# Five edits to a two-layer decoder trunk: order of the gate exponents, masks of the attention scores, last feed-forward chunk, first weight pieces, planned costs

## The chip, the cores and the metric

The kernel runs on one core of one Trainium2 chip. The metric is the device time of one execution in microseconds (us). A measurement of this kernel repeats to a few tenths of a microsecond: three runs of the kernel before gave 2133.31, 2133.43 and 2133.77 us.

## The reference

Input x is 256 tokens by 2048 features in float32. There are two layers. Each computes x + W_out(mixer(RMSNorm(x) W_in)) and then x + squared-ReLU MLP(RMSNorm(x)) with 8192 hidden features.

Layer 0's mixer is sparse attention with 16 heads of 128 in 4 groups. A query sees three branches: 15 compressed blocks of keys, selected blocks (with 256 tokens every block is selected, so this is plain causal attention) and a window (causal as well). Each branch has its own masked softmax, and a gate weighs the three.

Layer 1's mixer is gated linear attention (GLA) with 4 heads, 256 keys and 512 values per head:

```
log_a = log_sigmoid(g_lr @ w_gate_up + b_gate) / 16
decay = exp(cum_i - cum_j)        # cum: running sum of log_a, per key feature, j <= i
att   = einsum('id,jd,ijd->ij', q, k, decay);   o = att @ v  (+ state of earlier chunks)
o     = rms_norm(o) * silu(r)
```

## The kernel before, in words

**Precision.** Every large product is done with operands split into a high and a low fp32r part (hi, lo): hi·hi + hi·lo + lo·hi. For a piece of weights of 128 x 1024, ScalarE writes the high part (`copy`, L197, tile wh) and VectorE the low part (`tt`, L201, tile wl). TensorE multiplies with 512 columns at a time (`mm`, L166).

**Order of the work.** One stream of TensorE instructions is written out by the program: projections, feed-forward chunks, output projections. Weights come in halves; `Weights.next` (L491) splits up to three halves ahead of the one in use. All the small work in between (norms, softmax, decays, evacuations) lives in generators, "streams", that a planner steps. `Plan` (L34) keeps a modelled time per engine; each helper adds a planned cost (for example `free * 1.042 + 75` ns for a VectorE tensor_tensor). After each matmul `W.tick` (L98) goes through the streams in the order in which they were spawned and lets each that is ready emit its next step, unless ScalarE or VectorE is modelled over 3.2 us ahead of TensorE. `W.drain` and `W.wait` (L109, L116) step streams with no such bound until a stream is done or a buffer is free. Instructions are emitted in that order and each engine executes its own in order, so a planned cost that is too low makes TensorE wait at a product whose operand is late.

**NSA scores.** `attend` (L1331) handles one head: token tile 0 gets one PSUM tile of 272 columns (128 selected, 128 window, 16 compressed), token tile 1 one of 256 and one of 272. `score` (L1339) makes three products per tile and, for the two tiles of 272, a fourth, identity times mask, that adds 0 or -1e30. `largest` (L1358) takes the negated row maxima by VectorE (tensor_reduce), `ex` (L1361) the exponentials by ScalarE from PSUM, with the sum as a second output.

**GLA.** `decays` (L1551) makes log_a, `exponents` (L1601) builds for each head 8 levels of partial sums by copies (`keep`, L1597) and additions on VectorE and then exponentials; `attn` (L1670) multiplies them with q and k, makes the attention matrix and merges blocks with 20 copy_predicated (L1747, planned at 110 ns each); `head_out` (L1781) multiplies with the values. Heads are worked in two pairs; the second pair's buffers (`kq`) are waited for at its start. All four exponent streams are spawned before the streams of the first pair, so they come first in each tick.

**MLP.** The hidden features go in 8 chunks of 1024. For the down projection of chunks 0 to 6 two block pairs are done by a seven-product scheme (`Seven`, L879) in place of eight; the weights of a product are sums of blocks (`Group`, L305), made by GpSimd's adding DMA or, one (t2) in every second group and one (d2) in every group, by VectorE. Chunk 7 is done with eight plain products (`Plain`, L921; two block pairs are 16 halves of 12 matmuls each). `hidden` (L834) makes the activated planes, seven for the scheme, four for plain.

**Start.** The first two weight tiles come in six pieces (`load_first`, L403), 2 KB or 4 KB per partition cut from rows of 8 KB. The first twelve TensorE instructions are warm-up products on zeros.

Of the kernel before, what the change touches and what calls it, by code (L numbers as in the profile page):

```python
# [29 lines left out]
SEVENS = (2, 2, 2, 2, 2, 2, 2, 0)  # L30
# [3 lines left out]
class Plan:  # L34
# [49 lines left out]
    def spawn(self, gen):  # L84
        s = {"gen": gen, "ready": 0.0, "need": {}, "done": False}
        self.streams.append(s)
        self._step(s)
        return s
# [9 lines left out]
    def tick(self, slack=3200.0):  # L98
        taken = set()
        for s in list(self.streams):  # L100
# [8 lines left out]
    def drain(self, s, enough=lambda: False):  # L109
        while not s["done"] and not enough():  # L110
            before = [(id(q), q["ready"], q["need"]) for q in self.streams]
            self.tick(1e9)
            if before == [(id(q), q["ready"], q["need"]) for q in self.streams]:
                self.t["pe"] += 50.0

    def wait(self, needs):  # L116

        while not all(sum(f < 1e12 for f in self.slots[tag]) >= n for tag, n in needs.items()):
            self.tick(1e9)
# [4 lines left out]
def trunk_kernel(ctx: ExitStack, tc: tile.TileContext, a: dict, out: bass.AP):  # L124
# [231 lines left out]
    class Weights:  # L356
# [46 lines left out]
        def load_first(self, between):  # L403
# [4 lines left out]
            for j, (i, lo, hi) in enumerate(((0, 0, 512), (0, 512, 1024), (1, 0, 512), (1, 512, 1024), (0, 1024, 2048), (1, 1024, 2048))):  # L408
                nc.sync.dma_start(self.raws[i][:, lo:hi], self.units[i][0][:, lo:hi])  # L409
# [119 lines left out]
    MIXES = {0: "C" * 16, 2: "UU" + "SUSUSUSUSUUSUS" + "SUSUSUSUSUUSUS"}  # L529

    def mlp_items(c):
        return MIXES[SEVENS[c]]

    def mlp_units(layer):
# [8 lines left out]
        for c in range(8):  # L543
            down = a["mlp_down"][layer, c]
            n = {"U": 0, "S": 0, "C": 0}
            for it in mlp_items(c):
                i = n[it]
                n[it] += 1
                if it == "S":
                    if i % 7 == 0:  # L550
                        g = weights.group([down[i // 7, u] for u in range(4)])
                    weights.piece(g, Group.ORDER[i % 7])
# [4 lines left out]
                else:  # L557
                    if i % 2 == 0:
                        uc = weights.unit(down[SEVENS[c] + i // 8, i // 2 % 4])
# [184 lines left out]
    class PrepTokens(Prep):  # L744
# [3 lines left out]
        def start(self, b):  # L748
            if b == 0:
# [37 lines left out]
    def mlp(prep, after, last):  # L787
        op = prep.op
        with tc.tile_pool(name="mlpz", bufs=1) as zp:
# [20 lines left out]
            class Up:  # L810


                def __init__(self, c):
                    self.c = c
                    self.pairs = []
                    self.zz = None
                    self.pss = {}

                def half(self, f, half):
# [10 lines left out]
                    if f % 2 == 0:  # L830
                        self.pairs.append(pair_tile(c, f // 2))
                    last_z[:] = [W.spawn(self.hidden(ps, f))]

                def hidden(self, ps, f):  # L834
# [17 lines left out]
                    n = 7 if "S" in mlp_items(self.c) else 4  # L852
                    if n == 7:
                        both = pz[:, 0, :]
                        both = bass.AP(tensor=both.tensor, offset=both.offset,
                                       ap=[list(both.ap[0]), [3 * P, 2], [1, P]])
# [3 lines left out]
                    ht = self.pairs[f // 2][0]  # L860
# [18 lines left out]
            class Seven:  # L879
# [4 lines left out]
                def __init__(self, pairs, b):  # L884
# [4 lines left out]
                def product(self, name):  # L889
# [31 lines left out]
            class Plain:  # L921


                def __init__(self, c, pairs, first):
                    self.c, self.pairs, self.first = c, pairs, first

                def stationary(self, kt, t):
                    ht = self.pairs[kt // 2][0]
                    s = 2 * (kt % 2) + t
                    return ht[:, 0, s, :], ht[:, 1, s, :]  # L930

                def half(self, i):
# [3 lines left out]
                    if self.c == 7 and i == 0:  # L936
# [7 lines left out]
                    if self.c < 7:  # L944
                        return
                    if last:
                        for t in range(NT):
                            nc.sync.dma_start(out[t * P:(t + 1) * P, b * 512:(b + 1) * 512], xt[t][b])
                    if after is not None:
                        after.start(b)  # L950
# [14 lines left out]
            for c in range(8):  # L965
                items = mlp_items(c)
                nxt = Up(c + 1) if c < 7 else None
                plain = Plain(c, cur.pairs, 2 * SEVENS[c])
                n = {"U": 0, "S": 0, "C": 0}
                for it in items:  # L970
# [6 lines left out]
                    elif it == "S":  # L977
                        if i == 0:
                            hidden_done()
                        if i % 7 == 0:  # L980
                            seven = Seven(cur.pairs, 2 * (i // 7))
# [8 lines left out]
    def nsa(prep, after):  # L990
        op = prep.op
        G, HPG = 4, 4
        with tc.tile_pool(name="nsa1", bufs=1) as s1, tc.tile_pool(name="nsa2", bufs=1) as s2:
# [7 lines left out]
            def tables():  # L1001

                yield 20000.0, {"t4": 1}
                identr = s1.tile([P, P], F32R, name="identr")
                vcopy(identr, ident)
                maskf = t4([P, 288])
                nc.sync.dma_start(maskf, a["nsa_mask"])
                maskr = s1.tile([P, 288], F32R, name="maskr")
# [17 lines left out]
                cst.update(identr=identr, maskr=maskr, gcol=gcol, w2=w2, pe=pe, stack=stack, vsel=vsel)  # L1026
                yield 50000.0
                vcopy(maskr, maskf)
# [3 lines left out]
                W.give(maskf, W.t["dve"])  # L1032
# [298 lines left out]
            def attend(g, h, qT, oT, pair):  # L1331

                k = kT[g]
                maskr = cst["maskr"]
# [4 lines left out]
                def score(ps, lo, n, t, mask):  # L1339
# [11 lines left out]
                score(s0, 0, 272, 0, maskr[:, 16:288])  # L1351
# [16 lines left out]
                ex(0, s0[:, 256:272], nb0, 0, 0)  # L1368
                ex(32, s0[:, 0:128], nb0, 1, 1)
                ex(160, s0[:, 128:256], nb0, 2, 2)  # L1370
                W.give(s0, W.t["act"])
                yield 0.0, {"aux": 2}
                s1a, s1b = aux([P, 512]), aux([P, 512])
                score(s1a, 0, 256, 1, None)
# [7 lines left out]
                ex(16, s1b[:, 0:16], nb1, 0, 3)  # L1382
# [622 lines left out]
```

## Time and profile before

| | |
|---|---|
| median of 3 runs | 2133.43 us (2133.31 to 2133.77) |
| the profiled execution, its own time | 2133.26 us |
| its span, first to last instruction | 2131.5 us |
| TensorE (PE) busy | 2121.5 us |
| VectorE (DVE) busy | 1784.3 us |
| ScalarE (ACT) busy | 1358.4 us |
| GpSimd (POOL) busy | 154.9 us |
| mean granted TensorE clock | 0.999 |

The span falls into NSA (to about 395 us), the first MLP (to about 1066), GLA (to about 1460) and the second MLP. A matmul's record is longer than its share of the engine: records overlap, so the distance between starts is the price of one, not its duration. An idle time in brackets names who ended it.

### The profile page before, as it was taken

What the parts mean: (1) busy time and instruction counts of PE and PEld (TensorE: products, weight loads), DVE (VectorE), ACT (ScalarE), POOL (GpSimd) and SP (SyncE); (2) the same over time, 40 slices, a digit from 0 to 9 for tenths busy, and PEclk for the clock granted to TensorE, in tenths of its full rate; (3) what the DMA queues carried; (4) which work ended last, traced back from release to release, by engine and by line L of the source; (5) the groups of instructions that cost most, each with busy time, mean ns of one, the idle gap of its engine ahead of it and who ended that gap; (6) DMA issues with size and microseconds to landing.
All of it is one profiled execution on the core that took longest, in us unless ns stands there. A gap on an engine that the chain in (4) does not pass through costs nothing.

```text
span 2131.5 us, 29821 instructions
## 1 busy us (share of the span) xinstructions
PE 2121.5 (100%) x10971; PEld 1797.3 (84%) x10971; DVE 1784.3 (84%) x2626; ACT 1358.4 (64%) x2047; POOL 154.9 (7%) x184
## 2 busy tenths in 40 slices
PE   9999999999999999999999999999999999999999
PEld 7888888888888888888888788888888888888887
DVE  7778777789999999998658987667899999999985
ACT  6568676666667666666566564536666666667663
POOL 0010100000110011001000000000000100010010
PEclk9999999999999999999999999999999999999999
DMA  7554444769889879878645354556698898798784
GB/s 287 205 198 139 153 164 149 235 227 297 257 241 299 265 243 281 274 240 244 203 162 194 130 176 173 174 187 238 225 300 258 238 291 268 244 279 278 240 240 153
DMA packets 97826, 482.20 MB, mean 226 GB/s; under 512 B 12176, under 2 KB 12832, under 8 KB 64144
## 3 DMA queue, kind: packets, MB, share of 16 engines
q1 hardware_dynamic: 76320, 403.53, 52.2%
q0 software_dynamic: 21216, 76.51, 18.0%
q8 instruction: 86, 1.41, 0.2%
q14 instruction: 60, 0.49, 0.1%
q10 hardware_dynamic: 144, 0.26, 0.0%
HBM read 404.76 MB, written 2.10 MB: 191 GB/s over the span
## 4 chain that ended last, share of the span: by engine, by line
PE 98%; DVE 1%; DMA 0%; issue 0%; ACT 0%; SPq 0%; ACTq 0%
PE psa L166 59%; PE psx L166 37%; PE psx L170 2%; DVE wl L201 0%; DVE g L201 0%; DMA raw<-in_nsa_in_dram 0%; DVE att L1747 0%; DVE g L1599 0%; DVE laT L201 0%; DVE rest L201 0%; DVE g L205 0%; ACT wh L197 0%; DVE xt L205 0%; DVE ath L201 0%; SPq L409 0%
## 5 line engine op out<-in xcount | busy, mean ns | idle before, releaser
L166 PE MATMUL psa<-wh,op 128*128 128x512 f32 x2616 | 849.7, 393 | 0.2 <-ACT wh L197 0.2
L201 DVE TENSOR_TENSOR wl<-raw,wh 128x1024 fp32r<-128x1024 f32 (+1 forms) x530 | 643.1, 1218 | 182.3 <-ACT wh L197 171.3
L197 ACT CAST wh<-raw 128x1024 fp32r<-128x1024 f32 (+1 forms) x534 | 557.5, 1046 | 291.8 <-PE psa L166 260.5
L166 PEld LDWEIGHTS psa<-wh,op 128*128 128x128 f32 x2616 | 492.4, 188 | 102.6 <-ACT wh L197 0.6
L201 DVE TENSOR_TENSOR wl<-sraw,wh 128x1024 fp32r<-128x1024 f32 x392 | 473.5, 1220 | 52.4 <-ACT wh L197 47.3
L166 PE MATMUL psx<-op,wh 128*128 128x512 f32 (+1 forms) x2080 | 515.8, 390 | 0.0
L166 PE MATMUL psa<-wl,op 128*128 128x512 f32 x1308 | 511.2, 391 | 0.2 <-DVE wl L201 0.2
L197 ACT CAST wh<-sraw 128x1024 fp32r<-128x1024 f32 x392 | 412.2, 1053 | 152.4 <-PE psa L166 59.5
L166 PEld LDWEIGHTS psx<-op,wh 128*128 128x128 f32 (+1 forms) x2080 | 385.1, 188 | 77.8
L166 PE MATMUL psa<-wh,ht 128*128 128x512 f32 x1128 | 382.0, 391 | 0.0
L166 PEld LDWEIGHTS psx<-op,wl 128*128 128x128 f32 x2048 | 279.5, 191 | 20.0
L166 PEld LDWEIGHTS psa<-wl,op 128*128 128x128 f32 x1308 | 246.3, 188 | 48.5 <-DVE wl L201 0.8
L166 PE MATMUL psx<-op,wl 128*128 128x256 f32 x2048 | 286.2, 283 | 0.0
L166 PEld LDWEIGHTS psa<-wh,ht 128*128 128x128 f32 x1128 | 212.8, 189 | 39.0
L166 PE MATMUL psa<-wl,ht 128*128 128x512 f32 x564 | 221.7, 393 | 0.0
L338 POOL DMA_DIRECT2D sraw<-sraw x140 | 119.8, 920 | 1289.5 <-DVE pz L201 429.9
L205 DVE SCALAR_TENSOR_TENSOR xt<-psa,r,xt 128x512 f32<-128x512 f32 x212 | 157.4, 745 | 26.9 <-PE psa L166 26.1
L197 ACT COPY zz<-psx 128x256 f32<-128x256 f32 x128 | 47.6, 372 | 169.0 <-PE psx L166 168.8
L166 PEld LDWEIGHTS psa<-wl,ht 128*128 128x128 f32 x564 | 106.7, 189 | 15.3 <-DVE wl L201 0.4
L201 DVE TENSOR_TENSOR sraw<-sraw,sraw 128x1024 f32<-128x1024 f32 x84 | 102.6, 1221 | 1.0
L201 DVE TENSOR_TENSOR zz<-psx,zz 128x256 f32<-128x256 f32 x128 | 53.7, 419 | 13.6 <-ACT zz L197 13.6
L197 ACT CAST ht<-pz 128x896 fp32r<-128x896 f32 (+1 forms) x40 | 37.1, 928 | 14.6 <-DVE pz L205 13.5
(195 smaller groups left out, 1195.8 us busy)
## 6 DMA issues: line engine op xcount, KB each, us to landing
raw<-in_mlp_up_dram SPq DMA_DIRECT2D x128, 1024.0 KB, 7.5
sraw<-in_mlp_down_dram SPq DMA_DIRECT2D x224, 512.0 KB, 11.4
sraw<-sraw POOLq DMA_DIRECT2D x140, 512.0 KB, 9.5
raw<-in_gla_in_dram SPq DMA_DIRECT2D x48, 1024.0 KB, 4.9
raw<-in_nsa_in_dram SPq DMA_DIRECT2D x38, 1024.0 KB, 4.8
raw<-in_nsa_out_dram SPq DMA_DIRECT2D x16, 1024.0 KB, 4.8
raw<-in_mlp_down_dram SPq DMA_DIRECT2D x16, 1024.0 KB, 4.9
raw<-in_gla_out_dram SPq DMA_DIRECT2D x16, 1024.0 KB, 4.8
```

The source lines that it names most:

```text
L166: nc.tensor.matmul(dst, lhsT, rhs, skip_group_check=True, **kw)
L170: nc.tensor.transpose(dst, src, idn)
L197: nc.scalar.copy(dst, src)
L201: nc.vector.tensor_tensor(dst, x, y, op=op)
L205: nc.vector.scalar_tensor_tensor(dst, x, s, y, op0=op0, op1=op1)
L338: nc.gpsimd.dma_start(dst, src, accum_op=ALU.add)
```

## The change

Five edits. (1) The four exponent streams are marked `later`: in a tick they come after all other streams, and in `drain` and `wait` they get only the bounded tick. (2) The mask products go; VectorE adds the mask while it writes the negated scores to SBUF and takes the minimum (tensor_tensor_reduce, in the new helper `least`), and ScalarE exponentiates in place with scale -1. The mask tile no longer passes through one of the two `t4` buffers. (3) The last chunk of the second MLP does one of its two block pairs by seven products, in the order CC S C S C S C S C S C S C S, its t2 sum by DMA; each output block is sent when its last product is added. Its hidden planes are seven plus one pair (`over`) for the plain products. (4) The six first weight pieces are each contiguous in DRAM. (5) Planned costs: the copies of `exponents` are planned at the cost of `vcopy`, copy_predicated at 235 ns in place of 110.

```diff
-SEVENS = (2, 2, 2, 2, 2, 2, 2, 0)
+SEVENS = ((2, 2, 2, 2, 2, 2, 2, 0), (2, 2, 2, 2, 2, 2, 2, 1))
...
-    def tick(self, slack=3200.0):
+    def tick(self, slack=3200.0, later=True):
         taken = set()
-        for s in list(self.streams):
+        for s in sorted(self.streams, key=lambda s: s["later"]):
+            if s["later"] and not later:
+                return
             if max(self.t["act"], self.t["dve"]) > self.t["pe"] + slack:
                 return
...
-            self.tick(1e9)
+            self.tick(1e9, False)
+            self.tick()
...
+    def least(dst, x, y, acc):
+
+        W.run("dve", free(dst) * 1.042 + 150, [dst, acc], [x, y])
+        nc.vector.tensor_tensor_reduce(dst, x, y, scale=-1.0, scalar=3e38, op0=ALU.add, op1=ALU.min, accum_out=acc)
...
-                nc.sync.dma_start(self.raws[i][:, lo:hi], self.units[i][0][:, lo:hi])
+
+                flat = self.units[i][0].rearrange("p n -> (p n)")
+                nc.sync.dma_start(self.raws[i][:, lo:hi], flat[P * lo:P * hi].rearrange("(p c) -> p c", p=P))
...
-    MIXES = {0: "C" * 16, 2: "UU" + "SUSUSUSUSUUSUS" + "SUSUSUSUSUUSUS"}
+    MIXES = {0: "C" * 16, 1: "CCSCSCSCSCSCSCS", 2: "UU" + "SUSUSUSUSUUSUS" + "SUSUSUSUSUUSUS"}
...
                         g = weights.group([down[i // 7, u] for u in range(4)])
+                        if c == 7:
+                            g.odd = 1
...
+                        if sevens[c] == 1:
+                            if t[1] is not None:
+                                self.over.append(t[0][:, :, 7, :])
+                            else:
+                                self.over.append(zp.tile([P, 2, P], F32R, tag="over", name=nm("over")))
...
-                    n = 7 if "S" in mlp_items(self.c) else 4
+                    ht, over = self.pairs[f // 2][0], self.over[f // 2] if self.over else None
+                    if over is not None:
+
+                        copy(over[:, 0, :], pz[:, 1, :])
+                        yield W.ready(over)
+                        tt(over[:, 1, :], pz[:, 1, :], over[:, 0, :].bitcast(F32), ALU.subtract)
...
+                    n = 7 if sevens[self.c] else 4
...
+                        if self.c == 7 and name in ("b21", "t2", "d2", "t4"):
+                            finished(t, b + k)
...
-                    if self.c == 7 and i == 0:
+                    if i == 0:
                         hidden_done()
...
-                    if mask is not None:
-                        mm(dst, cst["identr"], mask, start=False, stop=False)
...
-                def ex(c0, src, nb_, br, i):
+                def masked(dst, c0, src, m):
+
                     n = src.shape[-1]
-                    act(p[:, c0:c0 + n], src, AF.Exp, bias=nb_[:, br:br + 1], acc=sums[:, i:i + 1])
-
-                largest(nb0[:, 0:1], s0[:, 256:272])
-                largest(nb0[:, 1:3], s0[:, 0:256].rearrange("p (b k) -> p b k", b=2))
+                    least(p[:, c0:c0 + n], src, m, dst)
+
+                def ex(c0, n, nb_, br, i, src=None):
+                    q = p[:, c0:c0 + n]
+                    act(q, q if src is None else src, AF.Exp, bias=nb_[:, br:br + 1],
+                        scale=-1.0 if src is None else None, acc=sums[:, i:i + 1])
+
+                masked(nb0[:, 0:1], 0, s0[:, 256:272], mask[:, 272:288])
+                for b in range(2):
+                    masked(nb0[:, 1 + b:2 + b], 32 + b * P, s0[:, b * P:(b + 1) * P], mask[:, 16:16 + P])
+                W.give(s0, W.t["dve"])
...
-                score(s1b, 256, 272, 1, maskr[:, 0:272])
+                score(s1b, 256, 272, 1)
                 W.give(qT)
-                largest(nb1[:, 0:1], s1b[:, 0:16])
+                masked(nb1[:, 0:1], 16, s1b[:, 0:16], mask[:, 0:16])
                 largest(mx[:, 0, :], s1a[:, 0:256].rearrange("p (b k) -> p b k", b=2))
-                largest(mx[:, 1, :], s1b[:, 16:272].rearrange("p (b k) -> p b k", b=2))
+                for b in range(2):
+                    masked(mx[:, 1, b:b + 1], 544 + b * P, s1b[:, 16 + b * P:16 + (b + 1) * P], mask[:, 16:16 + P])
...
-                        keep(second, uv[:, :, 1, :])
+                        vcopy(second, uv[:, :, 1, :])
                         if hs > 1:
-                            keep(first, av[:, :, 0, :])
+                            vcopy(first, av[:, :, 0, :])
...
-                        W.run("dve", 110.0, [att], [pl])
+                        W.run("dve", 235.0, [att], [pl])
...
-                        sums = sums + [W.spawn(exponents(hd, sums[-1], es[hd]))]
+                        sums = sums + [W.spawn(exponents(hd, sums[-1], es[hd]), True)]
```

The host's layout lays the down weights of that block pair and the six first pieces out to match.

## Rows read from the trace of the kernel before

**Rows 1.** The page: busy time by engine, and VectorE's busy tenths in 40 slices.

```profile
PE 2121.5 (100%) x10971; PEld 1797.3 (84%) x10971; DVE 1784.3 (84%) x2626; ACT 1358.4 (64%) x2047; POOL 154.9 (7%) x184
...
DVE  7778777789999999998658987667899999999985
```

**Rows 2.** The chain of waits in order of time: start, us, what.

```profile
2081.03 46.28 PE psa L166 x204
```

**Rows 3.** Waits of TensorE, 1200 to 1250 us: total us, times, longest.

```profile
PE psx L166 <- DVE ath L201: 2.7, 1, 2.7
PE psx L170 <- DVE g L205: 0.8, 2, 0.5
PE psx L166 <- DVE g L201: 0.6, 1, 0.6
```

**Rows 4.** Windows: busy us (instructions) of PE, PEld, DVE, ACT, POOL; PEclk, DMA share, GB/s.

```profile
1205.00:1210.00 5.00, 2.27 (x11) 1.55 (x9) 4.97 (x18) 2.92 (x5) 0.00 (x0) 1.00 0.34 82
1210.00:1215.00 5.00, 5.00 (x15) 3.97 (x16) 4.96 (x21) 1.38 (x4) 0.00 (x0) 0.66 0.31 131
```

**Rows 5.** The start, timeline of all engines and (first row) the chain of waits.

```profile
1.65 5.04 DMA raw<-in_nsa_in_dram
...
6.72 1.88 ACT L197 CAST wh<-raw 128x512 fp32r<-128x512 f32 x3 [1.75 <-DMA raw<-in_nsa_in_dram]
6.81 0.39 PE L166 MATMUL psa<-wh,op 128*128 128x512 f32 x1
7.39 0.50 PE L166 MATMUL psa<-wh,op 128*128 128x512 f32 x1 [0.20 <-ACT wh L197]
8.12 0.50 PE L166 MATMUL psa<-wl,op 128*128 128x512 f32 x1 [0.22 <-DVE wl L201]
```

**Rows 6.** Timeline of TensorE around one head's scores, 161 to 163 us.

```profile
161.85 0.29 PE L166 MATMUL psx<-maskr,identr 128*128 128x272 f32 x1
161.97 0.54 PE L166 MATMUL psx<-kT,qT 128*128 128x272 f32 x3
```

**Rows 7.** Groups of instructions by line and shape, whole span: xcount | busy us, mean ns.

```profile
L166 PE MATMUL psx<-maskr,identr 128*128 128x272 f32 x32 | 9.2, 288 | 0.0
...
L220 DVE TENSOR_REDUCE mx<-psx 128x2 f32<-128x256 f32 x32 | 11.9, 414 | 0.0
L220 DVE TENSOR_REDUCE nb<-psx 128x1 f32<-128x16 f32 x32 | 5.4, 170 | 12.9 <-PE psx L166 12.9
L1661 DVE CUSTOM_DVE_ANT_0 dj<-g,g 128x256 f32<-128x256 f32 x8 | 3.4, 423 | 0.2
L1661 DVE DVE_READ_ACCUMULATOR2_ANT dg<- 128x1 f32 x8 | 0.7, 83 | 0.0
```

**Rows 8.** Windows, 100 to 395 us, the sum of six stretches.

```profile
sum 295.00, PE 295.00 PEld 249.18 DVE 229.55 ACT 205.03 POOL 21.15; mean PE 49.17 PEld 41.53 DVE 38.26 ACT 34.17 POOL 3.53
```

**Rows 9.** Timeline of ScalarE and VectorE where the last chunk begins, 2078 to 2087 us.

```profile
2078.93 1.05 ACT L197 CAST wh<-sraw 128x1024 fp32r<-128x1024 f32 x1 [3.27 <-DMA sraw<-sraw]
...
2085.35 0.62 ACT L197 CAST op<-pz 128x512 fp32r<-128x512 f32 x1
2086.00 0.69 DVE L201 TENSOR_TENSOR op<-pz,op 128x512 fp32r<-128x512 f32 x1 [0.23 <-ACT op L197]
```

**Rows 10.** Groups by line and shape: the low part of seven hidden planes.

```profile
L201 DVE TENSOR_TENSOR op<-pz,op 128x896 fp32r<-128x896 f32 x18 | 19.6, 1087 | 0.0
```

**Rows 11.** Timeline of VectorE in GLA, 1197 to 1211 us.

```profile
1198.90 4.71 DVE L1747 COPY_PREDICATED att<-lmask,psx 64x32 f32<-64x32 uint8 x20
...
1204.78 0.22 DVE L1599 COPY g<-laT 128x128 f32<-128x128 f32 x1
...
1209.34 0.56 DVE L201 TENSOR_TENSOR ath<-att,ath 128x384 fp32r<-128x384 f32 x1
```

**Rows 12.** Groups by line and shape: half of the four heads' exponents on VectorE.

```profile
L201 DVE TENSOR_TENSOR laT<-g,laT 128x128 f32<-128x128 f32 x56 | 16.0, 286 | 0.3
L1599 DVE COPY g<-laT 128x128 f32<-128x128 f32 x64 | 13.7, 214 | 0.0
```

More of the change, by code (lines that the diff above doesn't have):

```diff
@@ L118, in wait @@
         while not all(sum(f < 1e12 for f in self.slots[tag]) >= n for tag, n in needs.items()):
-            self.tick(1e9)
+            self.tick(1e9, False)
+            self.tick()
             self.t["pe"] += 50.0
@@ L545, in mlp_units @@
             n = {"U": 0, "S": 0, "C": 0}
-            for it in mlp_items(c):
+            for it in mlp_items(layer, c):
                 i = n[it]
@@ L748, in start @@
         def start(self, b):
-            if b == 0:
+            if self.sum is None:
                 self.sum = small.tile([P, NT, NB], F32, tag="ssq", name=nm("ssq"))
@@ L788, in mlp @@
         op = prep.op
+        layer = int(last)
+        sevens = SEVENS[layer]
         with tc.tile_pool(name="mlpz", bufs=1) as zp:
@@ L815, in __init__ @@
                     self.pairs = []
+                    self.over = []
                     self.zz = None
@@ L921, in mlp, with __init__ @@
             class Plain:
-                def __init__(self, c, pairs, first):
-                    self.c, self.pairs, self.first = c, pairs, first
+                def __init__(self, c, up, first):
+                    self.c, self.pairs, self.over, self.first = c, up.pairs, up.over, first
                 def stationary(self, kt, t):
@@ L929, in stationary @@
                     s = 2 * (kt % 2) + t
+                    if s == 1 and self.over:
+                        over = self.over[kt // 2]
+                        return over[:, 0, :], over[:, 1, :]
                     return ht[:, 0, s, :], ht[:, 1, s, :]
@@ L943, in half, with finished @@
                         W.give(self.ps[t], W.t["dve"])
-                    if self.c < 7:
-                        return
-                    if last:
+                    if self.c == 7:
                         for t in range(NT):
-                            nc.sync.dma_start(out[t * P:(t + 1) * P, b * 512:(b + 1) * 512], xt[t][b])
-                    if after is not None:
-                        after.start(b)
+                            finished(t, b)
+            def finished(t, b):
+                if last:
+                    nc.sync.dma_start(out[t * P:(t + 1) * P, b * 512:(b + 1) * 512], xt[t][b])
+                elif t == 1:
+                    after.start(b)
             last_z = []
@@ L980, in mlp @@
                         if i % 7 == 0:
-                            seven = Seven(cur.pairs, 2 * (i // 7))
+                            seven = Seven(c, cur.pairs, 2 * (i // 7))
                         seven.product(Group.ORDER[i % 7])
@@ L1001, in tables @@
             def tables():
-                yield 20000.0, {"t4": 1}
+                yield 20000.0
                 identr = s1.tile([P, P], F32R, name="identr")
                 vcopy(identr, ident)
-                maskf = t4([P, 288])
-                nc.sync.dma_start(maskf, a["nsa_mask"])
-                maskr = s1.tile([P, 288], F32R, name="maskr")
+                mask = s1.tile([P, 288], F32, name="mask")
+                nc.sync.dma_start(mask, a["nsa_mask"])
                 cs = zpool.tile([P, NT, 2, 32], F32, tag="gz", name="cs")
@@ L1333, in attend @@
                 k = kT[g]
-                maskr = cst["maskr"]
+                mask = cst["mask"]
                 yield W.ready(qT, k), {"aux": 1, "p": 1}
@@ L1337, in attend, with score @@
                 p = ptile([P, 800])
-                def score(ps, lo, n, t, mask):
+                def score(ps, lo, n, t):
                     qh = qT[:, 0, t * P:(t + 1) * P]
@@ L1625, in exponents @@
                             else:
-                                keep(av[:, :, 0, :], second)
+                                vcopy(av[:, :, 0, :], second)
                         if l % 4 == 0:
@@ L1897, in _units_down, with _pieces @@
     u = plain.copy()
-    for c, n in enumerate(SEVENS):
-        u[:, c, :n] = seven[:, c, :n]
+    for layer in range(2):
+        for c, n in enumerate(SEVENS[layer]):
+            u[layer, c, :n] = seven[layer, c, :n]
+    return u
+def _pieces(u):
+    u = u.copy()
+    for b in range(2):
+        u[b, 0] = np.concatenate([u[b, 0, :, lo:hi].ravel() for lo, hi in ((0, 512), (512, 1024), (1024, 2048))]).reshape(P, 2048)
     return u
```

61 lines of the change are left out of this document (28 added, 33 removed).

## The prediction

> **What bounds the kernel now.** First the page's busy times: TensorE is busy 2121.5 us of a span of 2131.5 us, VectorE 1784.3 us [rows 1]. So the time is TensorE's stream of products plus the few places where it stands still, and an edit is worth what it takes out of that stream or out of those places. Second the chain of waits, for the price of one product: 204 matmuls of 512 columns in a row take 46.28 us, 0.227 us each, start to start [rows 2]. Third the list of TensorE's waits: nearly all of it lies in GLA between 1200 and 1250 us, where TensorE waits 2.7 us for the low part of the attention matrix (ath), 0.8 us for a scaled output tile and 0.6 us for a product with the exponents (g), always for VectorE [rows 3]. The windows there show VectorE busy 4.97 us of 5, and TensorE's granted clock at 0.66 in the five microseconds after the long wait [rows 4]. Last the start, where the second piece of weights is late [rows 5].
>
> The profiled execution took 2133.26 us, 0.17 us under the median of 2133.43 us; the sum is made against 2133.26 and 0.17 us is added at its end. A measurement of this kernel can tell a difference of about 0.2%, 4.3 us.
>
> **Masks by VectorE.** 32 mask products go, two for each of 16 heads [rows 7]. One costs the distance to the next start, 161.85 to 161.97 us, 0.12 us, which is near 272/512 of 0.227 us; 0.125 us taken [rows 2, 6]. TensorE waits nowhere in that stage (295.00 us busy of 295.00, [rows 8]), so the whole of 32 x 0.125 = 4.0 us leaves the path.
>
> What pays is VectorE. A head had three reductions of 256 columns (414 ns) and two of 16 (170 ns): 1.58 us [rows 7]. It now has one of 256, four tensor_tensor_reduce of 128 and two of 16. The only row of that instruction has 256 columns, 423 ns, and a read of the accumulator, 83 ns [rows 7]. Its fixed part I take from the two reductions, (414 - 170)/240 = 1.02 ns a column, so 128 columns cost 423 - 130 + 83 = 0.38 us and 16 columns 0.26 us; the head 0.41 + 1.50 + 0.52 = 2.43 us, 0.85 us more, 13.6 us for 16 heads. VectorE is busy 229.55 us of 295 there [rows 8]; 65 us idle cover it. The cover is thinner locally: each head's exponentials now start up to 0.85 us later in two portions, and the planner books a 128-column instruction at 283 ns. Bounds: nothing, or every portion shown, 13.6 us. The nearest row is the absence of any wait there today, so 0.3 us is taken. The mask's buffer comes free earlier and the score tiles are returned before the exponentials; both only loosen waits, and there are none.
>
> **GLA's exponents.** Two things made ath late. The 20 copy_predicated before it took 4.71 us, 235 ns each, against 110 ns planned, so VectorE fell 2.5 us behind the plan; and steps of a later head's exponents stand between them and ath (copies from 1204.78 us on, ath's low part at 1209.34 us) [rows 11]. The change puts the right cost in and the exponents last. What can go: the waits, 2.7 + 0.8 + 0.6 = 4.1 us [rows 3], and the slow clock behind them, (1 - 0.66) x 5 = 1.7 us [rows 4], together 5.8 us; a record outlasts its price by some 0.16 us (0.39 against 0.227), which hides as much at each of the four waits, so at most 6.4 us. At least nothing goes, or the wait moves to the next head. Taken: 5.4 us, since the plan error alone is nearly the long wait, and the two short ones are its echo. VectorE has room before: 5 and 8 tenths in the two slices from 1066 to 1172 us, 9 in the next [rows 1], so heads 0 and 1 find their time early.
>
> **Seven products in the last chunk.** Two block pairs cost 16 halves of 12 = 192 matmuls; now one costs 96 and the other 7 x 12 = 84. Twelve matmuls less are 12 x 0.227 = 2.7 us [rows 2], all on the path, since TensorE is busy to the end. Against it: the chain of the last hidden pair is longer. It ended with the low part at 2086.00 + 0.69 us [rows 9]; with seven planes that instruction takes 1.09 us [rows 10], ScalarE's split grows likewise (0.62 us for four planes, some 0.95 for seven), and the pair `over` and the three plane differences add about 1.5 us, estimated from the same per-column cost; it ends near 2089.0 us. The last pair is needed in the second half of b11: the last product of chunk 6 begins at 2081.0 us, so CC begins at 2083.7, b11 at 2089.1, its fourth pair at 2091.1 us. It is in time by 2 us, but the splits of the weights for b11 stand behind the chain on both engines, since `hidden_done` now emits it whole before the first C. Bounds 0 and 2 us; 0.4 us taken. The adding DMA for t4 may be late too: today ScalarE waited 3.27 us for one [rows 9], hidden by the halves split ahead, and nothing is queued behind the last t4 but its own halves; 0. SP issues eight half tiles in place of four whole ones, the same bytes, and GpSimd's queue six adds more; both queues are hidden by the same lead as in the chunks before. The end itself, one addition and one store behind the last matmul, keeps its form.
>
> **First pieces contiguous.** The second piece takes 5.04 us from issue to landing; the starts 6.81, 7.39 and 8.12 us hold two products that should take 0.45 us and took 1.31 us, so at most 0.9 us is to be had; before 6.1 us the warm-up products hold TensorE anyway [rows 5]. Bounds 0 and 0.9, 0.5 taken, because the pieces behind it must come earlier as well.
>
> A rule speaks against this edit: the Trainium skill, "DMA: Bandwidth & Descriptors", section Specifications, gives 512 B as the least transfer at line rate, and the pieces had 2 KB before and have it still. By that rule the term is 0 and the time 0.5 us later. The trace's long landing speaks for something beyond it, but not for what.
>
> **Sum.** -4.0 + 0.3 - 5.4 - 2.7 + 0.4 - 0.5 = -11.9 us; 2133.26 - 11.9 + 0.17 = **2121.5 us**.
>
> **Rivals.** *The GLA wait only moves.* The exponents still enter in every tick that has room, and a later head's ath or transposes meet them instead. For it: VectorE is full in that slice whatever the order [rows 1]. Against: with right costs the planner places the product later, and a drain now steps the exponents only within the bound. It gives back 5.4 us: 2126.9 us. Chance 0.14.
>
> *VectorE shows through in NSA.* If a third of the 13.6 us comes out as waits (plan 283 ns against 380), 4.5 us return: 2125.7 us. For it: margins of a quarter microsecond in the plan; against: no wait today. Chance 0.07.
>
> *Slower: the exponents come too late.* Pushed behind everything, head 1's exponents are not yet emitted when the second pair begins (the wait for `kq` in `gla`); the planner's clock runs on, and TensorE later waits for them. One head costs VectorE (16.0 + 13.7)/4 = 7.4 us for the sums on laT and nearly as much on rest (one level of eight less): 13.9 us [rows 12]. With the GLA gain lost, -6.5 + 13.9 + 1.7 (slow clock) = +9.1: 2142.5 us. It decides if more than the slack of the first slices is missing; the room in them [rows 1] speaks against it. Chance 0.04.
>
> *The edits don't do what they say*: masks and products are counted from the code, so this concerns the order and the pieces alone, and is the first rival.
>
> **How the numbers follow.** The forecast has 0.71, the first two rivals 0.21, several small givebacks together (a result within 0.2%) 0.04, the slower one 0.04. Faster is 0.71 + 0.21 = 0.92. The range's lower end takes every term at its best: -4.0 - 6.4 - 2.7 - 0.9 = -14.0, 2119.4 us, and about 1.5 us for waits hidden inside records elsewhere: 2118.0. Its upper end takes in the first rival: 2127.0 us.
>
> **What would show it.** Right: no mask product in NSA and no new waits of TensorE there; in the list of waits no ath entry in GLA, clock 1.00 throughout; in the last chunk 180 matmuls, shorter by 2.7 us; the second piece landing under 4 us. Wrong: TensorE waiting for VectorE between 150 and 395 us, a wait of microseconds in GLA at another head, or one for wh or wl at the first b11 of the last chunk.

## The result, and the profile after

The changed kernel takes **2120.18 us** (median of 6 runs, 2119.40 to 2121.49) where the kernel before took 2133.48 us (6 runs beside it, 2133.31 to 2133.90): a ratio of **0.9938, 95% interval 0.9925 to 0.9951**, 13.3 us less. The profiled execution took 2120.32 us with a span of 2118.5 us. Line numbers are those of each kernel; lines 166, 170, 197, 201 and 205 of the kernel before are 171, 175, 202, 206 and 210 in the changed one.

The page's busy times, changed kernel:

```profile
PE 2112.0 (100%) x10927; PEld 1788.4 (84%) x10927; DVE 1802.4 (85%) x2780; ACT 1369.0 (65%) x2057; POOL 154.2 (7%) x190
```

TensorE is busy 9.5 us less than in [rows 1], and its own 44 products less are the 32 of the masks and the 12 of the last chunk. VectorE took on 18.1 us, and the kernel is faster all the same.

All of TensorE's waits in the changed kernel (total us, times, longest):

```profile
PE psx L171 <- DVE idle L306: 1.2, 1, 1.2
PE psx L175 <- ACT g L202: 0.7, 1, 0.7
PE psa L171 <- DVE wl L206: 0.5, 1, 0.5
```

The first is the start, before anything can run, and the kernel before has it too. Of the three waits of [rows 3] none is left; a new one of 0.7 us, on ScalarE, stands in front of the transposes at 1218 us. The one of 0.5 us is at 17.7 us; five runs without this edit of the start have it too, at 0.2 to 0.7 us. The windows of [rows 4] and the one behind them, changed kernel:

```profile
1205.00:1210.00 5.00, 5.00 (x24) 4.14 (x23) 5.00 (x12) 3.89 (x6) 0.00 (x0) 1.00 0.59 210
1210.00:1215.00 5.00, 4.97 (x117) 4.01 (x116) 5.00 (x17) 0.52 (x1) 0.00 (x0) 1.00 0.01 3
1215.00:1220.00 5.00, 4.31 (x20) 3.12 (x19) 4.96 (x21) 4.02 (x12) 0.00 (x0) 1.00 0.82 246
```

VectorE (third busy time) is as full as it was. What changed is what it does first: TensorE (first busy time) is fed, and the granted clock (behind the five busy times) is 1.00 throughout. The chain of waits (start, us, what) gives the anchors by which the saving can be placed. The kernel before:

```profile
395.22 47.97 PE psx L166 x276
...
1461.68 47.97 PE psx L166 x276
```

The changed kernel:

```profile
390.42 47.97 PE psx L171 x276
...
1451.55 47.97 PE psx L171 x276
...
2071.05 43.56 PE psa L171 x192
```

The two pieces of 276 products lie at the same place of the first and of the second MLP. The first came 4.80 us earlier (395.22 - 390.42): start and NSA. From the first to the second took 1061.13 us for 1066.46: GLA, 5.33 us. The last piece has 192 products and 43.56 us where [rows 2] had 204 and 46.28: 2.72 us. Sum 12.85 us of the 12.94 us between the two profiled executions. How well such distances repeat is seen in runs that share the code of a stretch: the first MLP starts at 395.03 to 395.58 us in the six traces with the old start and masks, and from the first MLP to the second it takes 1066.45 to 1067.10 us in the four with the old GLA, 1060.91 to 1061.13 us in the three with the new.

### The profile page after: what moved, and what is told of

Read it like the earlier page. It is cut to its first block, busy times and chain, and to the rows that moved or that the text cites. A ratio compares the mean times of both kernels' runs of the same rounds, so it can differ in the third digit from the quotient of the medians.

```text
span 2118.5 us, 29932 instructions
## 1 busy us (share of the span) xinstructions
PE 2112.0 (100%) x10927; PEld 1788.4 (84%) x10927; DVE 1802.4 (85%) x2780; ACT 1369.0 (65%) x2057; POOL 154.2 (7%) x190
## 4 chain that ended last, share of the span: by engine, by line
PE 97%; DVE 1%; ACT 0%; DMA 0%; issue 0%; SPq 0%; DVEq 0%; ACTq 0%
PE psa L171 59%; PE psx L171 37%; PE psx L175 2%; DMA xs<-in_x_dram 0%; DVE wl L206 0%; DVE g L206 0%; ACT wh L202 0%; SPq L421 0%; DVE g L210 0%; ACT p L198 0%; DVE g L221 0%; DVE op L210 0%; ACT op L198 0%; DVE xt L210 0%; DVE xt L206 0%
## 5 line engine op out<-in xcount | busy, mean ns | idle before, releaser
L206 DVE TENSOR_TENSOR wl<-raw,wh 128x1024 fp32r<-128x1024 f32 (+1 forms) x522 | 633.0, 1216 | 166.9 <-ACT wh L202 152.9
L202 ACT CAST wh<-raw 128x1024 fp32r<-128x1024 f32 (+1 forms) x526 | 549.1, 1045 | 264.2 <-PE psa L171 238.8
L206 DVE TENSOR_TENSOR wl<-sraw,wh 128x1024 fp32r<-128x1024 f32 x406 | 490.0, 1217 | 48.4 <-ACT wh L202 44.7
L202 ACT CAST wh<-sraw 128x1024 fp32r<-128x1024 f32 x406 | 427.0, 1053 | 153.6 <-PE psa L171 68.7
L348 POOL DMA_DIRECT2D sraw<-sraw x146 | 125.3, 932 | 1323.4 <-DVE pz L206 467.2
L206 DVE TENSOR_TENSOR sraw<-sraw,sraw 128x1024 f32<-128x1024 f32 x86 | 104.9, 1220 | 1.0
```

The costliest lines, as they stand in the source:

```text
L202: nc.scalar.copy(dst, src)
L206: nc.vector.tensor_tensor(dst, x, y, op=op)
L348: nc.gpsimd.dma_start(dst, src, accum_op=ALU.add)
```

## Experiments

Each was timed in three rounds beside the kernel before, whose median was 2133.4 to 2133.7 us in every comparison. The four parts alone come first, GLA's in two halves.

**Masks alone.** The parts of the edit on the mask and in `attend` only, cut to the first tile:

```diff
-                score(s0, 0, 272, 0, maskr[:, 16:288])
+                score(s0, 0, 272, 0)
...
-                largest(nb0[:, 0:1], s0[:, 256:272])
-                largest(nb0[:, 1:3], s0[:, 0:256].rearrange("p (b k) -> p b k", b=2))
+                masked(nb0[:, 0:1], 0, s0[:, 256:272], mask[:, 272:288])
+                for b in range(2):
+                    masked(nb0[:, 1 + b:2 + b], 32 + b * P, s0[:, b * P:(b + 1) * P], mask[:, 16:16 + P])
```

> The kernel before with the masks by VectorE alone. Theory (the products leave the path whole, VectorE's part is hidden): 3.7 to 4.1 us shorter, TensorE without waits over 0.3 us between 150 and 395 us. Rival (VectorE shows through): 0 to 2.5 us shorter, waits of TensorE for VectorE or ScalarE in that stretch.

2129.33 us (2128.74 to 2130.45), ratio 0.9981 (0.9971 to 0.9990): 4.4 us less, where 32 products of 0.125 us are 4.0 us. Its chain reaches the first MLP 4.36 us earlier:

```profile
390.86 47.97 PE psx L166 x276
```

That is 0.136 us for each product, and it repeats only as well as the start does. In GLA the wait for ath is still 2.7 us; the wait for g (L201) is 2.2 us for 0.6, and the way from the first MLP to the second 0.64 us longer. The kernel with the seven products alone, whose GLA is that of the kernel before, shows the same wait of 2.2 us, so it isn't put down to the masks.

**VectorE's masks twice.** The changed kernel with one line doubled, so that every masked minimum is executed and planned twice (the second writes what the first wrote):

```diff
                     least(p[:, c0:c0 + n], src, m, dst)
+                    least(p[:, c0:c0 + n], src, m, dst)
```

> The changed kernel with every masked minimum executed (and planned) twice, 96 more products with their reads. In the changed kernel they keep VectorE busy for 29.2 us (15.8 + 5.4 + 5.3 + 2.7) between 158 and 340 us, where it is busy for 0.79 of the time; twice as many bring it to 0.95 there. Theory (VectorE's part is covered, only TensorE's part counts): the first MLP starts at 387.1 to 388.1 us, total 2120 to 2121 us. Rival (the masks are near the edge of VectorE's cover and the next 29 us show through): TensorE waits for p or for nb in that stretch, 3 us or more, total 2123 to 2130 us. Second rival (all of it on the path): about 2149 us.

2132.33 us (2130.86 to 2136.46), 12 us slower than the changed kernel. First what one set costs, groups by line and shape of the changed kernel (count, busy us, mean ns, then the idle time before them):

```profile
L230 DVE CUSTOM_DVE_ANT_0 p<-psx,mask 128x128 f32<-128x128 f32 x64 | 15.8, 284 | 0.0
L230 DVE CUSTOM_DVE_ANT_0 p<-psx,mask 128x16 f32<-128x16 f32 x32 | 5.4, 168 | 5.6 <-PE psx L171 5.6
L230 DVE DVE_READ_ACCUMULATOR2_ANT nb<- 128x1 f32 x64 | 5.3, 82 | 0.0
L230 DVE DVE_READ_ACCUMULATOR2_ANT mx<- 128x1 f32 x32 | 2.7, 83 | 0.0
```

29.2 us together. With the 16 reductions that are left (6.7 us) this is 35.9 us, where all reductions of the kernel before took 11.9 + 6.6 + 5.4 = 23.9 us: the masks cost VectorE 12.0 us net. TensorE's waits with twice as many masked minima:

```profile
PE psx L175 <- ACT p L198: 2.5, 1, 2.5
PE psx L171 <- DVE pT L206: 2.3, 2, 1.8
...
PE psx L175 <- DVE p L206: 0.8, 1, 0.8
PE psa L171 <- ACT op L202: 0.7, 1, 0.7
...
```

Two windows (busy us of PE, PEld, DVE, ACT, POOL; clock, DMA share, GB/s):

```profile
300.00:350.00 50.00, 50.00 (x252) 42.29 (x251) 45.48 (x144) 33.16 (x96) 0.00 (x0) 1.00 0.43 146
350.00:390.00 40.00, 33.51 (x162) 26.60 (x161) 26.35 (x70) 19.95 (x51) 0.00 (x0) 0.91 0.29 96
```

The last head's products with the values, first in the changed kernel, then with twice as many:

```profile
356.21 2.28 PE L171 MATMUL psx<-pT,vv 128*128 128x512 f32 x12
```

```profile
370.76 4.35 PE L171 MATMUL psx<-pT,vv 128*128 128x512 f32 x12
```

The theory that VectorE's part stays covered falls, and the time is 2 us above even the first rival's range. Up to 350 us TensorE is busy without a gap. From 350 us on it is busy 33.51 us of 40, at a granted clock of 0.91; the last head's products stand 14.6 us later, with TensorE's waits in front of them, and take nearly twice as long; the first MLP comes 11.0 us later (401.46 us in its chain for 390.42). A reading that fits: a head that ends later costs nothing while the planner still has projections to put in front of it, and shows once these are used up. The first 29.2 us on VectorE came free, and the next set cost 11 us. The run doubles the planned cost together with the work, so it doesn't tell a busier VectorE from the later order that the planner then chose. The average (VectorE 232.52 us of 295.00 from 100 to 395 us in the changed kernel) doesn't show that edge.

**GLA: the planned durations alone.** What the planner books for the exponents' copies (three places) and for the predicated copy, no change of order in the turns:

```diff
-                        keep(second, uv[:, :, 1, :])
+                        vcopy(second, uv[:, :, 1, :])
...
-                        W.run("dve", 110.0, [att], [pl])
+                        W.run("dve", 235.0, [att], [pl])
```

> The kernel before with the planned costs alone (copies of the exponents as vcopy, copy_predicated at 235 ns); the exponents keep their place in the order. Theory A (the plan's error made ath late): the wait for ath in GLA falls from 2.7 us to under 0.5 us, the clock stays at 1.00, the time is 4 to 6 us shorter. Theory B (the exponents' place in the order made it late): the wait stays at 2 us or more and the time within 1 us of before.

2136.03 us (2135.62 to 2136.89), ratio 1.0011 (1.0002 to 1.0021): **2.3 us slower**, which neither theory said. The predicated copy is now booked dearer, 235 ns for 110; the exponents' copies are booked cheaper, 128 columns at 143 ns (0.53 a column and 75) for 208. The wait for ath is gone, and a longer one stands 10 us behind it, in front of the head's transposes. TensorE's timeline there, kernel with the planned durations alone:

```profile
1207.08 2.21 PE L166 MATMUL psx<-g,ath 128*128 128x512 f32 x9
...
1217.45 1.47 PE L170 MATMUL psx<-cid,g 128*128 128x128 f32 x4 [6.79 <-DVE g L205]
```

VectorE's timeline in front of it, same kernel (the first row begins a run of 14 instructions of the exponents that ends with the second):

```profile
1211.32 0.22 DVE L216 COPY g<-laT 128x128 f32<-128x128 f32 x1
1211.45 0.22 DVE L216 COPY g<-rest 128x128 f32<-128x128 f32 x1
...
1213.48 0.22 DVE L216 COPY g<-rest 128x128 f32<-128x128 f32 x1
1213.61 0.16 DVE L212 TENSOR_SCALAR oss<-oss 128x2 f32<-128x2 f32 x1
1213.68 2.77 DVE L201 TENSOR_TENSOR g<-g,kq 128x256 f32<-128x256 f32 x8
1216.36 0.15 DVE L201 TENSOR_TENSOR ro<-ro,rhalf 128x2 f32<-128x2 f32 x1
1216.55 1.41 DVE L205 SCALAR_TENSOR_TENSOR g<-psx,ro,g 128x512 f32<-128x512 f32 x2
```

The two copies start 0.13 us apart, so 143 ns is near what they take. TensorE waits for the last row; a later head's exponents hold VectorE for 2.3 us, and eight multiplications by the exponents (`g<-g,kq`) for 2.8 us more, ahead of it. The clock in this stretch averages 0.90 over 50 us (0.97 in the kernel before).

**GLA: the predicated copy's duration alone**, to see which of the booked durations does it:

```diff
-                        W.run("dve", 110.0, [att], [pl])
+                        W.run("dve", 235.0, [att], [pl])
```

> The kernel before with one planned duration alone: the predicated copy at 235 ns for 110. Theory (the prediction's reading: the plan's error on this copy is the long wait for ath): the wait for ath goes as it did with both planned durations, and the loss seen there (6.8 us for g in front of the transposes) came with the exponents' dearer copies, so that it stays out: total 2130.5 to 2132 us. Rival (any correct duration pushes the plan over into the other order): the wait for ath goes and one of 5 to 7 us for g comes, total 2135.5 to 2137 us. Second rival (it is the copies' duration that took ath's wait away): waits as in the kernel before, total 2133 to 2134 us.

2135.94 us (2135.41 to 2136.80), ratio 1.0012 (1.0003 to 1.0021): 2.5 us slower, with neither of the expected pictures. The wait for ath not only stays, it grows:

```profile
1211.06 1.22 PE L166 MATMUL psx<-g,ath 128*128 128x512 f32 x2 [4.50 <-ACT ath L197]
1214.14 3.35 PE L166 MATMUL psx<-g,ath 128*128 128x512 f32 x7 [1.86 <-DVE ath L201]
```

VectorE's timeline of the same kernel shows why: the 20 predicated copies are split, sixteen at 1198.70 and the last four, on which ath hangs, at 1209.43 us, with exponents between and behind them.

```profile
1198.70 3.67 DVE L1747 COPY_PREDICATED att<-lmask,psx 64x32 f32<-64x32 uint8 x16
...
1209.43 0.93 DVE L1747 COPY_PREDICATED att<-lmask,psx 64x32 f32<-64x32 uint8 x4
...
1213.53 0.56 DVE L201 TENSOR_TENSOR ath<-att,ath 128x384 fp32r<-128x384 f32 x1
```

The planner had this copy's right duration and still let the exponents in ahead. So that copy's wrong duration was not the cause of the wait. (The expectation calls the exponents' copies of the run before dearer; they were booked cheaper, and with them cheaper too the wait moved from ath to g at the same total time.)

**GLA: the order alone**, with the old durations:

```diff
-            for s in list(self.streams):
+        for s in sorted(self.streams, key=lambda s: s["later"]):
...
-            self.tick(1e9)
+            self.tick(1e9, False)
+            self.tick()
```

> The kernel before with the exponents put last and bounded in drain and wait, old planned costs. Theory A: copy_predicated is still planned 2.5 us too short for a head, so a wait of 1.5 to 3 us for ath stays somewhere in GLA and less than 2 us is gained. Theory B: the wait is gone and 4 to 6 us are gained.

2129.90 us (2129.51 to 2130.61), ratio 0.9982 (0.9973 to 0.9992): 3.8 us less. Its waits:

```profile
PE psx L175 <- ACT g L202: 1.3, 1, 1.3
PE psx L171 <- DVE g L206: 1.3, 1, 1.3
PE psx L171 <- DVE idle L301: 1.2, 1, 1.2
PE psa L171 <- ACT wh L202: 0.6, 1, 0.6
PE psa L171 <- DVE wl L206: 0.2, 1, 0.2
```

The ath wait and the low clock (now 1.00) go with the order; four small waits remain beside the one at the start. VectorE's timeline shows what the rank does:

```profile
1186.48 1.75 DVE L1752 COPY_PREDICATED att<-lmask,psx 64x32 f32<-64x32 uint8 x8
...
1196.76 0.55 DVE L206 TENSOR_TENSOR ath<-att,ath 128x384 fp32r<-128x384 f32 x1
```

Exponents still stand between the predicated copies and ath, but all of it begins 12 us earlier than in [rows 11] (1186.48 for 1198.90, ath 1196.76 for 1209.34).

**GLA: order and durations together**, on the kernel before:

> Both GLA parts (the rank of the exponents' streams and the planned durations) on the kernel before, nothing else. Theory (the planned durations alone are worth a loss, but with the lower rank they are worth the rest of the 5.3 us by which GLA is shorter in the changed kernel; the parts aren't additive): total 2128.0 to 2128.9 us, waits in GLA of 1.2 us together at most 3, TensorE at its full clock. Rival (rank and durations add: -3.8 and +2.3): about 2132.2 us. Second rival (the rank is all, the durations do nothing behind it): 2129.5 to 2130.3 us.

2128.00 us (2127.77 to 2128.94), ratio 0.9975 (0.9964 to 0.9985): 5.5 us less, with one wait of 0.7 us in GLA. The parts are not additive (-3.8 and +2.3 would make -1.5): durations that alone cost 2.3 us are worth 1.7 us once the exponents come last. The two 95% intervals overlap; no run of either kernel reaches into the other's (2129.51 to 2130.61 against 2127.77 to 2128.94).

**GLA: which half of the order.** The rank acts in two places: in each turn, and in the waits that force work out. First the turn keeps the old order and only the forced waits are bounded:

```diff
-        for s in sorted(self.streams, key=lambda s: s["later"]):
+        for s in list(self.streams):
             if s["later"] and not later:
-                return
+                continue
```

> The changed kernel, but in an ordinary turn the exponents' streams keep their place in the list instead of coming last; the forced waits still leave them to the bounded turn. Theory A (the bound in the forced waits is what matters): no wait over 1.5 us in GLA, total 2119.5 to 2121.5 us. Theory B (the place in each turn matters, the exponents' copies stand in front of the head's own VectorE work): a wait of 2 to 4 us for g or ath in the second pair, total 2122 to 2125 us.

2129.38 us (2127.98 to 2131.45): 9.2 us of the changed kernel's 13.3 lost again, more than either theory allowed. In the trace 8.0 us of this lie between the first products of the two MLPs (1457.04 - 387.88 against 1448.23 - 387.10).

```profile
1202.72 2.21 PE L171 MATMUL psx<-g,ath 128*128 128x512 f32 x9
...
1213.75 1.47 PE L175 MATMUL psx<-cid,g 128*128 128x128 f32 x4 [7.46 <-DVE g L210]
```

It is the picture of the planned durations alone, but for the end of the wait, where VectorE itself stood 0.6 us for GpSimd:

```profile
1212.66 0.16 DVE L206 TENSOR_TENSOR ro<-ro,rhalf 128x2 f32<-128x2 f32 x1 [0.59 <-POOL ro L238]
```

In the changed kernel the same product with ath stands at 1190.46 us, 12 us earlier. Then the other half: last in each turn, but unbounded where work is forced out:

```diff
-            self.tick(1e9, False)
-            self.tick()
+            self.tick(1e9)
```

> The changed kernel, but the exponents' streams are drained without bound wherever the head's planes are waited for (they still come last in each turn, and the planned durations stay). Theory A (the bound in the forced waits is what took the burst away from in front of the second pair of heads): the burst comes back as in the run with the planned durations alone, a wait of 5 to 7 us for g or kq before the transposes, and with TensorE's clock at its half level behind it the total is 2125 to 2128 us. Theory B (it is enough that the exponents come last in each turn): no wait over 1.5 us in GLA, total 2119.5 to 2121.5 us.

2121.86 us (2120.73 to 2122.48), ratio 0.9944 (0.9930 to 0.9959), longest wait in GLA 1.3 us. The burst does not come back. The interval overlaps that of the changed kernel, so what the bound adds (1.7 us by the medians, 2.0 us between the two MLPs in the traces) isn't settled; the place in each turn carries the part. Both halves were taken out with the new durations only.

**Seven products alone.** `SEVENS` by layer, the mix for one pair, `over`, and `finished`:

```diff
-SEVENS = (2, 2, 2, 2, 2, 2, 2, 0)
+SEVENS = ((2, 2, 2, 2, 2, 2, 2, 0), (2, 2, 2, 2, 2, 2, 2, 1))
```

> Only the second layer's last chunk in seven products for its first pair of column blocks, with its sums by DMA, on the kernel before. Theory (four products of TensorE are saved, and the sums by DMA end before the last plain block does): the second MLP is shorter by 2.3 to 2.9 us, total 2130.8 to 2131.4 us; no wait of TensorE behind 2070 us, and the last instruction is still VectorE's addition into xt. Rival 1 (the prediction's own give-back, new addends and copies late for the first products): a wait of 0.4 us or more at the chunk's first product, total 2131.2 to 2131.6. Rival 2 (the last sums by DMA, 5 us each, end the kernel): the last row is a DMA's and the total is 2133 or more.

2130.86 us (2130.39 to 2131.51), ratio 0.9987 (0.9977 to 0.9997): 2.7 us less, 12 products of 0.227 us and nothing given back. No wait of TensorE lies behind 1250 us.

**Seven products in the first layer's last chunk too**, on the changed kernel, in search of more. Their mix is `"CSCSCSCSCSSSCCC"` (S a product of the seven, C half a plain unit):

```diff
-SEVENS = ((2, 2, 2, 2, 2, 2, 2, 0), (2, 2, 2, 2, 2, 2, 2, 1))
+SEVENS = ((2, 2, 2, 2, 2, 2, 2, 1), (2, 2, 2, 2, 2, 2, 2, 1))
```

> The changed kernel with the same seven products and sums by DMA in the last chunk of the first layer's MLP too, its products placed so that three half units of the plain blocks come behind the last one. Theory (what pays in the second layer is TensorE's time alone): the first MLP is shorter by 2.3 to 2.9 us, the sums by DMA (5.4 to 5.9 us each) are over when GLA's first projections want the normed blocks, total 2117.3 to 2118.2 us. Rival (GLA's preparation of the first two column blocks, which are now finished last, comes late: sum of 5.5 us, then squares, transposes and splits): a wait of 3 to 8 us for op at GLA's start, with TensorE's clock at its half level behind it, total 2122 to 2128 us.

2123.20 us (2122.52 to 2124.17), 3.0 us slower than the changed kernel, but not for the rival's reason: GLA's first products don't wait for op. TensorE's waits from 1000 to 1070 us:

```profile
PE psa L171 <- DVE xt L210: 3.7, 2, 2.4
PE psa L171 <- DVE wl L206: 0.4, 1, 0.4
```

and the windows there:

```profile
1030.00:1040.00 10.00, 10.00 (x50) 8.34 (x49) 10.00 (x13) 5.32 (x9) 0.85 (x1) 1.00 0.33 91
1040.00:1050.00 10.00, 6.32 (x27) 4.66 (x26) 8.65 (x10) 6.55 (x10) 1.86 (x3) 1.00 0.38 71
```

VectorE, busy 10.00 of 10 us from 1030 to 1040 us, splits the sevens' weights and sums and prepares GLA's input at once; the addition that empties an accumulator queues behind it, and TensorE waits for the accumulator. Another mix might spread this; none was tried.

**First pieces alone.** The weights of the first two units stored so that each piece is one contiguous block:

```diff
-                nc.sync.dma_start(self.raws[i][:, lo:hi], self.units[i][0][:, lo:hi])
+                flat = self.units[i][0].rearrange("p n -> (p n)")
+                nc.sync.dma_start(self.raws[i][:, lo:hi], flat[P * lo:P * hi].rearrange("(p c) -> p c", p=P))
```

> The kernel before with the six first pieces contiguous alone. Theory: the second piece lands under 4 us after its issue (5.0 before), the two late products of the start lose their wait, 0.5 to 1 us shorter. Rival (2 KB pieces are at line rate either way, the landing is set by something else): landing within 0.5 us of before, time within 0.3 us of before.

2132.66 us (2132.00 to 2133.30), ratio 0.9995 (0.9986 to 1.0004): 1.0 us by the medians, which the interval can't tell from nothing; the chain reaches the first MLP 0.44 us earlier (394.78 us). Issues of the four pieces of 2 KB per partition, with the median time from issue to landing, the kernel before and then the changed one:

```profile
raw<-in_nsa_in_dram SPq DMA_DIRECT2D x4, 256.0 KB, 5.1
```

```profile
raw<-in_nsa_in_dram SPq DMA_DIRECT2D x4, 256.0 KB, 3.6
```

These two lie near the ends of what the traces show. The second piece to be issued took 5.04 us in the kernel before and 3.31 us in the changed one, but 3.9 to 5.0 us over all seven traces with the old layout (mean 4.5) and 3.2 to 4.3 us over all six with the new (mean 3.7): some 0.8 us sooner in the mean, and single executions overlap. The two gaps of 0.2 us of [rows 5] are likewise no sure mark: three of the seven traces with the old layout start without them, and one of the six with the new has one.

By the medians the four parts alone sum to -4.4 - 5.5 - 2.7 - 1.0 = -13.6 us, the whole is -13.3 us: as far as this can tell, they don't touch one another.

## Why the prediction was right, and where its reasons were not

The forecast was 2121.5 us, 1.3 us above the measurement, in the direction and near the size of each term.

**What bounds the kernel: right.** Time left only where TensorE's products or its waits left; 18.1 us more on VectorE cost nothing that TensorE's waits show.

**Masks, -4.0 + 0.3: right in the first, 0.3 too much in the second.** The masked minimum of 128 columns was put at 0.38 us with its read and took 284 + 82 ns, 0.37 us; the one of 16 columns 168 + 83 ns for 0.26 us; the net price on VectorE was 12.0 us for the 13.6 forecast. TensorE is busy 294.90 of 295.00 us in that stage (295.00 in [rows 8]), so the give-back was at most 0.1 us there. The first MLP came 4.36 us earlier with the masks alone, so 4.0 was 0.4 us too little, as far as the start repeats. But "65 us idle cover it" was a poor reason: in the run with doubled masks the first MLP comes 11 us later, while the same count of idle time would still have covered the second set. What covers, as that run is read here, is the other work that TensorE still has while the last heads end.

**GLA, -5.4: the size right, the reason wrong.** GLA gave 5.33 us in the profile, 5.5 us alone. The step that failed is "the plan error alone is nearly the long wait, and the two short ones are its echo". With the predicated copy's duration put right alone the long wait grew from 2.7 to 6.4 us (4.50 + 1.86); with all durations right it went and one of 6.8 us came in its place. In its place the runs show that the exponents, spawned before the head's streams, stood ahead of them in every turn, and that coming last takes the ath wait away, with the old durations as with the new, because the head's own work comes 12 us earlier; right durations then remove about 1.7 us of small waits. Nor were the short waits an echo of the long one: with the order alone the ath wait is gone and two of 1.3 us stay. The clock term was rightly joined to the wait: 1.00 from 1200 to 1250 us in every kernel without a wait over 1.4 us there, 0.90 to 0.97 in the others.

**The rival "the wait only moves"** describes the planned durations alone and the kernel whose turns keep the old order, at 6.8 and 7.5 us. It was priced at 5.4 us given back; the second of these gives back 9.2, 8.0 of them in GLA, and with right durations. Had the rank been only a bound in the forced waits, as the rival's counter-argument read it ("a drain now steps the exponents only within the bound"), the rival's mechanism would have held. **The slower rival** didn't show: no wait for the exponents of the second pair.

**Seven products, -2.7 + 0.4: -2.7.** The end of the last hidden pair's chain, timeline of ScalarE and VectorE, changed kernel:

```profile
2077.02 0.94 ACT L202 CAST op<-pz 128x896 fp32r<-128x896 f32 x1 [1.35 <-DVE pz L210]
...
2077.99 1.09 DVE L206 TENSOR_TENSOR op<-pz,op 128x896 fp32r<-128x896 f32 x1 [1.01 <-ACT op L202]
```

It ends at 2079.08 us (2077.99 + 1.09). The prediction's 2089.0 us is on the clock of the kernel before, whose last piece of the chain of waits began 9.98 us later (2081.03 us for 2071.05): on the clock of the changed kernel it is 2079.0 us. So the estimate of the chain's length held, and the 2 us of margin with it; the 0.4 us for splits queued behind the chain wasn't needed.

**First pieces, -0.5: near the size, as far as it can be told.** The first MLP comes 0.44 us earlier with the pieces alone, and 0.44 us earlier in the changed kernel than with the masks alone (390.42 for 390.86); the start itself repeats only to 0.55 us, and the 1.0 us of the medians can't be told from nothing. The Trainium skill, "DMA: Bandwidth & Descriptors", section Specifications, would have had the term at 0, since 2 KB is above its least size before and after. The mean landings, 4.5 us before and 3.7 us after with the same 2 KB for each partition, disagree; that the kernel's time does is not shown.

**Too few gains in sum:** the terms add to 11.9 us and the profiles show 12.85 us. Of the difference 0.7 us are give-backs that didn't come and 0.4 us the mask products; the other terms are off by under 0.1 us each.

## What to carry to other kernels

When work with a far deadline shares an engine with work that is wanted now, its rank in the queue decides, and correct durations in the planner can make a wrong rank worse: test order and durations apart, then together. An engine's idle time over a stage is no proof of cover; ask what the engine on the path still has to do when the last of the added work ends. Here 4 us of TensorE's products, moved to 12 us of a busy but not limiting engine, paid in full. One profile of each kernel is not enough to read a start by: look at the same stretch in every run that shares its code.

## What the runs showed that was not expected

A booked duration that was made right (235 ns for 110) and nothing else slowed the kernel by 2.5 us, the wait for ath going from 2.7 to 6.4 us. Where TensorE had stood for 7.5 us, its granted clock fell to near the lower of its two levels (1.2 GHz of 2.4): in the kernel whose turns keep the old order it was 0.53 from 1210 to 1215 and 0.79 from 1215 to 1220 us. Its way from the first MLP to the second is 8.0 us longer than the changed kernel's, whose own wait there is 0.7 us, so this wait cost more than itself.

```profile
1210.00:1215.00 5.00, 1.13 (x5) 0.86 (x5) 4.37 (x13) 1.42 (x2) 2.63 (x1) 0.53 0.00 0
1215.00:1220.00 5.00, 5.00 (x116) 4.29 (x114) 4.27 (x9) 1.89 (x3) 0.00 (x0) 0.79 0.45 138
```
